# A pitch of 520 columns for buffers of 512: neighbours at different addresses modulo 128 bytes

## The chip, the cores and the metric

The kernel runs on one core of a Trainium2 chip. The metric is the device time of one execution in microseconds. The core has a matrix engine (TensorE: PE in the profile, with its weight loads as PEld), three engines that work on vectors (VectorE: DVE, ScalarE: ACT, GpSimd: POOL) and a queue for transfers (SyncE: SP). They share an on-chip memory of 128 partitions, the SBUF; an address in it is a byte offset within a partition, the same for all 128. TensorE writes to a memory of its own, the PSUM, from which the other engines read.

## The reference

One layer of a hybrid encoder on x of 512 tokens by 2,048 features, all in float32:

```
h = RMSNorm(x);  [q k v u v_sgu gate_a gate_b] = h @ w_in          (2048 x 9216)
branch A: stick-breaking attention, 8 heads of 128, causal, in blocks of 128;  y_a = o @ w_oa
branch B: s = gelu(u) * (W_s LayerNorm(gelu(v_sgu)) + b), in chunks of 128;    y_b = s @ w_ob
x = x + (sigmoid(gate_a) * y_a + sigmoid(gate_b) * y_b) @ w_out
x = x + relu(RMSNorm(x) @ w_ff1)^2 @ w_ff2                          (hidden 8192)
```

## The kernel before

Every large product is made of float32r matmuls in three parts: each operand is split into a rounded part `hi` and a rest `lo`, and `mm3` adds hi x hi, hi x lo and lo x hi (lines 64, 65 and 66). A matmul has a stationary operand of 128 x 128 (loaded by an LDWEIGHTS ahead of it) and a moving operand of 128 partitions by up to 512 columns.

**Buffers.** Two pools of the SBUF hold nearly all that matmuls read:
- 81 *slots* of 512 float32 columns (2,048 bytes), handed out by `slot`. Whatever has 128 x 512 elements is in a slot: the normalised and split activations (`hT_hi`, `hT_lo`, `mT`, `h2T`, `ys` and the like), gates, `relu`, the residual `x2T`, scratch.
- 6 *pieces* of 1,024 columns (4,096 bytes), under the tag `w_piece`: the split weights `w_hi` and `w_lo`, and in `strassen` the sums `w_sum` and the split weights `w_both` (hi in one half, lo in the other).

The raw weights land by DMA in 3 buffers `w_raw` of 1,024 columns. Before the slots and pieces lie small constants, among them the 128 x 128 identity. In the built program the pieces start at byte 34,400 and the slots at byte 60,256, both 96 more than a multiple of 128.

**Work.** `weight` loads a piece of 256 x 512 (for `w_ff1` 512 x 256) weights, copies it to `w_hi` on ScalarE (line 86) and takes `w_lo` as the difference on VectorE (line 88). `by_token` uses slots as the stationary operand and pieces as the moving one; `by_column` the other way about. Both issue 24 matmuls of 512 columns per piece: they make the input projection (q, k, v, ga, vg, u, gb in the profile), `w_oa` (ya), `w_ob` (yb), `w_out` (xo) and `w_ff1` (f). The second product of the MLP is made in 64 blocks by `strassen`: 1,024 x 256 weights in quarters, so seven products of quarters instead of eight, with sums of weights made on GpSimd (line 156, `w_sum`), splits on ScalarE and VectorE (`split_to`, lines 99 and 100, `w_both`), 84 matmuls of 256 columns (q<-ys,w_both), and eight additions of the results to `x2T` on VectorE (line 624). The MLP goes in 8 chunks of 1,024 hidden columns: four pieces of `w_ff1` work (`hidden`), `factors` (sums of activations on GpSimd, split into `ys`) and 8 blocks of `strassen` each; they make up the second half of the time. Small pieces of work between the matmuls (attention, gating, transposes) come from the queue `behind`, one step per weight piece. A list scheduler sets the order of instructions on each engine.

Of the kernel before, what the change touches and what calls it, by code (L numbers as in the profile page):

```python
# [9 lines left out]
F32 = mybir.dt.float32  # L10
F32R = mybir.dt.float32r
# [4 lines left out]
P = 128  # L16
# [7 lines left out]
GROUPS = 8  # L24
DFF = 4 * D
EPS = 1e-6
CK = 2
W = 512

# [2 lines left out]
def tile_hybrid_layer(ctx: ExitStack, tc: tile.TileContext, x, g_mix, w_in, g_q, g_k, ln_g, ln_b,  # L32
# [7 lines left out]
    wpool = ctx.enter_context(tc.tile_pool(name="wpool", bufs=3))  # L40
    small = ctx.enter_context(tc.tile_pool(name="small", bufs=8))
    slots = ctx.enter_context(tc.tile_pool(name="slots", bufs=81))
# [1 line left out]
    ps_aux = ctx.enter_context(tc.tile_pool(name="ps_aux", bufs=3, space=bass.MemoryType.PSUM))  # L44

    def slot(name, dt=F32):
        return slots.tile([P, 512], dt, name=name, tag="slot")

    def acc(name):
        return ps_acc.tile([P, 512], F32, name=name, tag="acc")  # L50

    def aux(name):
        return ps_aux.tile([P, 512], F32, name=name, tag="aux")

    def tiny(n, name):
        return small.tile([P, n], F32, name=name, tag=f"tiny{n}")

    def f32(ap):
        return ap.bitcast(F32)


    def mm3(o, lh, rh, start, stop, **kw):

        nc.tensor.matmul(o, lhsT=lh[0], rhs=rh[0], start=start, stop=False, **kw)  # L64
        nc.tensor.matmul(o, lhsT=lh[0], rhs=rh[1], start=False, stop=False, **kw)  # L65
        nc.tensor.matmul(o, lhsT=lh[1], rhs=rh[0], start=False, stop=stop, **kw)  # L66
# [4 lines left out]
    def step():  # L71
        if behind:
            behind.popleft()()

    def flush():
        while behind:
            step()

    def weight(wap, kt, c0, w=W):

        ck = CK * W // w
        raw = wpool.tile([P, ck, w], F32, name="w_raw", tag="w_raw", bufs=3)
        state["load"] = nc.sync.dma_start(
            out=raw, in_=wap[kt * P:(kt + ck) * P, c0:c0 + w].rearrange("(k p) c -> p k c", p=P))
        hi = wpool.tile([P, ck, w], F32R, name="w_hi", tag="w_piece", bufs=6)
        nc.scalar.copy(out=hi, in_=raw)  # L86
        lo = wpool.tile([P, ck, w], F32R, name="w_lo", tag="w_piece", bufs=6)
        nc.vector.tensor_tensor(out=lo, in0=raw, in1=f32(hi), op=ALU.subtract)  # L88
        return hi, lo

    def split(src, name, scale=None):

        hi, lo = slot(name + "_hi", F32R), slot(name + "_lo", F32R)
        split_to(hi, lo, src, scale)
        return hi, lo

    def split_to(hi, lo, src, scale=None):
        if scale is None:
            nc.scalar.copy(out=hi, in_=src)  # L99
            nc.vector.tensor_tensor(out=lo, in0=src, in1=f32(hi), op=ALU.subtract)  # L100
        else:
            nc.scalar.activation(out=hi, in_=src, func=AF.Copy, scale=scale)
            nc.vector.scalar_tensor_tensor(out=lo, in0=src, scalar=scale, in1=f32(hi),
                                           op0=ALU.mult, op1=ALU.subtract)
# [3 lines left out]
    def by_token(wap, c0, lhs, nk, evac, name):  # L108

        o = [acc(name) for _ in range(NTB)]  # L110
        for kt in range(0, nk, CK):
            hi, lo = early.pop() if early else weight(wap, kt, c0)
            for tb in range(NTB):
                for k in range(CK):
                    a = [part[:, tb * P:(tb + 1) * P] for part in lhs(kt + k)]
                    mm3(o[tb], a, (hi[:, k, :], lo[:, k, :]), kt + k == 0, kt + k == nk - 1)
            step()
        for tb in range(NTB):
            evac(tb, o[tb])

    def by_column(wap, c0, rhs, nk, evac, name, w=W):

        o = [acc(name) for _ in range(w // P)]
        ck = CK * W // w
        for kt in range(0, nk, ck):
            hi, lo = weight(wap, kt, c0, w)
            for c in range(w // P):
                for k in range(ck):
                    a = [part[:, k, c * P:(c + 1) * P] for part in (hi, lo)]
                    mm3(o[c], a, rhs(kt + k), kt + k == 0, kt + k == nk - 1)  # L130
            for _ in range(ck // CK):
                step()
        for c in range(w // P):
            evac(c, o[c])

    def strassen(wap, r0, c0, rhs, evac):

        KH = 4
        half = []
        for h in range(2):
            raw = wpool.tile([P, KH, 2, P], F32, name="w_raw", tag="w_raw", bufs=3)
            state["load"] = nc.sync.dma_start(
                out=raw.rearrange("p k h c -> p k (h c)"),
                in_=wap[r0:r0 + 2 * KH * P, c0:c0 + 2 * P].rearrange("(k h p) c -> h p k c", p=P, h=2)[h])
            half.append(raw)  # L150
        w11, w21 = half[0][:, :, 0, :], half[0][:, :, 1, :]
        w12, w22 = half[1][:, :, 0, :], half[1][:, :, 1, :]
        sums = [wpool.tile([P, 2, KH, P], F32, name="w_sum", tag="w_piece", bufs=6) for _ in range(2)]
        sa, sc, sd, sb = sums[0][:, 0], sums[0][:, 1], sums[1][:, 0], sums[1][:, 1]
        for o, a, b in ((sa, w11, w21), (sc, sa, w22), (sd, sc, w12), (sb, w21, w22)):
            nc.gpsimd.tensor_tensor(out=o, in0=a, in1=b, op=ALU.add)  # L156
        banks = [acc("q") for _ in range(4)]
        for w, name, b, first, last in ((w11, "y11", 0, True, False), (w12, "y21", 1, True, True),
                                        (sa, "m7", 2, True, False), (sc, "m6", 0, False, False),
                                        (sd, "y22", 3, True, True), (w22, "m4", 2, False, True),  # L160
                                        (sb, "m5", 0, False, True)):
            both = wpool.tile([P, 2, KH, P], F32R, name="w_both", tag="w_piece", bufs=6)
            split_to(both[:, 0], both[:, 1], w)
            o = banks[b][:, :2 * P]
            for k in range(KH):
                mm3(o, (both[:, 0, k, :], both[:, 1, k, :]), rhs(k, name), first and k == 0, k == KH - 1,
                    skip_group_check=True)
            evac(name, o)
# [21 lines left out]
    def rsqrt(ms, n, name):  # L190

        r = tiny(n, name)
        nc.gpsimd.tensor_tensor(out=r, in0=ms, in1=mhalf[:, :n], op=ALU.pow)
        return r
# [25 lines left out]
    def load_xk(kt):  # L220

        t = slot("xk")
        nc.sync.dma_start(out=t.rearrange("p (b c) -> p b c", b=NTB),
                          in_=x[:, kt * P:(kt + 1) * P].rearrange("(b p) c -> p b c", p=P))
        for tb in range(NTB):
            xq[tb, kt] = t[:, tb * P:(tb + 1) * P]
        xq[kt] = t

    def load_x(q):

        for tb in range(NTB):
            t = slot("xq")
            nc.sync.dma_start(out=t, in_=x[tb * P:(tb + 1) * P, q * 512:(q + 1) * 512])
            for c in range(4):
                xq[tb, 4 * q + c] = t[:, c * P:(c + 1) * P]
            xq["r", tb, q] = t
# [23 lines left out]
    def scale_of_x():  # L260
        ms = tiny(4, "ms")
        nc.vector.tensor_reduce(out=ms, in_=ss, axis=AX.X, op=ALU.add)
        nc.vector.tensor_scalar(out=ms, in0=ms, scalar1=1.0 / D, scalar2=EPS, op0=ALU.mult, op1=ALU.add)
        nc.gpsimd.tensor_tensor(out=rstd, in0=ms, in1=mhalf, op=ALU.pow)
# [12 lines left out]
    turn_gains(gm, gT)  # L277
    load_xk(1)
    early.append(weight(w_in[0], 0, 0))
    load_xk(2)  # L280
    load_xk(3)
# [12 lines left out]
    def heads_of(c0, g0, half, name):  # L294
# [3 lines left out]
        def evac(tb, o):  # L298
# [6 lines left out]
                                    op=ALU.add)  # L305
            nc.vector.tensor_scalar(out=m, in0=m, scalar1=1.0 / P, scalar2=EPS, op0=ALU.mult,
                                    op1=ALU.add)
# [119 lines left out]
    with tc.issue_after(ref.ins):  # L427
        for half in range(2):
            for src, dst, nm in ((ln_g, lng, "lng"), (ln_b, lnb, "lnb")):
                t = slot(nm)  # L430
# [4 lines left out]
    def normed(tb):  # L435
# [5 lines left out]
        ve = tiny(1, "ve")  # L441
        nc.vector.tensor_scalar(out=ve, in0=mv[:, 1:2], scalar1=EPS, scalar2=None, op0=ALU.add)
        r = rsqrt(ve, 1, "r")
# [23 lines left out]
    with tc.issue_after(ref.ins):  # L467
        ws, bs = [], []
        for half in range(2):
            t = slot("ws")  # L470
# [3 lines left out]
            t = slot("bs")  # L474
# [65 lines left out]
    for j in range(D // W):  # L540
# [7 lines left out]
        with tc.issue_after(ref.ins):  # L548
            for tb in range(NTB):
                t = slot("x2")  # L550
# [17 lines left out]
    nc.vector.tensor_reduce(out=ms2, in_=ss2, axis=AX.X, op=ALU.add)  # L568
    nc.vector.tensor_scalar(out=ms2, in0=ms2, scalar1=1.0 / D, scalar2=EPS, op0=ALU.mult, op1=ALU.add)
    rstd2 = rsqrt(ms2, 4, "rstd2")  # L570
# [38 lines left out]
    for f in range(chunks):  # L609
# [5 lines left out]
        for j in range(D // (2 * P)):  # L615
# [11 lines left out]
            if f == chunks - 1:  # L627
                for pb in range(2):
                    t = aux("xo")
# [36 lines left out]
```

## Time and profile before

| | us |
|---|---|
| median of three timed runs | 2593.71 (2592.04 to 2594.72) |
| the profiled execution's own time | 2592.95 |
| its span, first to last instruction | 2591.2 |
| TensorE busy with matmuls | 2572.0 |
| VectorE / ScalarE / GpSimd busy | 1399.7 / 906.7 / 606.6 |

The lines of the profile are quoted where they are used. A group's row reads: line, engine, operation, written tile <- read tiles, shapes, count | busy time in us, mean ns of one | idle time of the engine just before them, and what ended it. A row of the waits reads: who waited for whom, us in total, times, longest. A row of the windows gives, for a stretch of the span in us, its length, the busy time and count of instructions of the engines shown, the granted TensorE clock, the share of time in which the DMA engines moved data, and GB/s. A row of the timeline gives start and length in us, and in square brackets how long the engine had been idle. Matmul durations include what it takes to get through the array, so they overlap; the spacing of starts is their pace.

### The profile page before, as it was taken

Reading aid. Unit: us, or ns where it says so; the run is one execution under the profiler, and the core shown is the slowest. Engines: PE = TensorE matmul, PEld = TensorE weight load, DVE = VectorE, ACT = ScalarE, POOL = GpSimd, SP = SyncE. Lnnn points to the kernel's source line nnn. Section 1 sums busy time; section 2 is a strip of 40 time slices with the busy share of each in tenths; the row PEclk is TensorE's granted clock in tenths of the full one; section 3 lists DMA queues with packets and bytes.
Section 4 is the critical chain, followed back from the end, with each engine's and each line's share of the span. In section 5 each row is a group of like instructions: output and inputs, shape, how many; then the busy total and the mean of one; then the engine's idle time right before and its main releaser. Section 6 shows DMA issues by size and latency. Waiting matters only on the chain.

```text
span 2591.2 us, 34954 instructions
## 1 busy us (share of the span) xinstructions
PE 2572.0 (99%) x14058; PEld 2235.7 (86%) x14058; DVE 1399.7 (54%) x2030; ACT 906.7 (35%) x1428; POOL 606.6 (23%) x507
## 2 busy tenths in 40 slices
PE   8999999999999999999999999999999999999999
PEld 7888888888888888888899898898998988989989
DVE  4555563333335333333567486584774856847666
ACT  5333342222223222233333343343333433433334
POOL 0211110000201100000143252351522624415233
PEclk9999999999999999999999999999999999999999
DMA  5332322333332333433333333233232332333333
GB/s 171 90 90 74 90 72 91 97 98 98 114 112 84 98 98 98 129 107 107 97 86 115 93 90 114 84 104 110 87 114 90 99 113 83 115 98 90 112 90 117
DMA packets 204419, 260.24 MB, mean 100 GB/s; under 512 B 8368, under 2 KB 146656, under 8 KB 204256
## 3 DMA queue, kind: packets, MB, share of 16 engines
q1 hardware_dynamic: 204256, 258.01, 33.3%
q8 instruction: 110, 1.80, 0.3%
q14 instruction: 53, 0.43, 0.1%
HBM read 253.78 MB, written 4.19 MB: 100 GB/s over the span
## 4 chain that ended last, share of the span: by engine, by line
PE 97%; DVE 2%; issue 0%; DMA 0%; ACT 0%; SPq 0%; POOL 0%; DVEq 0%; ACTq 0%; POOLq 0%
PE q L64 9%; PE q L66 9%; PE q L65 9%; PE f L65 9%; PE f L66 9%; PE f L64 9%; PE xo L66 2%; PE xo L64 2%; PE xo L65 2%; PE gb L64 2%; PE gb L65 2%; PE gb L66 2%; PE ga L64 2%; PE ga L66 2%; PE ga L65 2%; PE v L66 1%
## 5 line engine op out<-in xcount | busy, mean ns | idle before, releaser
L88 DVE TENSOR_TENSOR w_lo<-w_raw,w_hi 128x1024 fp32r<-128x1024 f32 x336 | 415.4, 1236 | 826.5 <-ACT w_hi L86 813.1
L86 ACT CAST w_hi<-w_raw 128x1024 fp32r<-128x1024 f32 x336 | 353.6, 1052 | 951.5 <-PE f L65 248.4
L64 PE MATMUL q<-ys,w_both 128*128 128x256 f32 x1792 | 505.4, 285 | 3.0 <-DVE x2T L624 0.6
L65 PE MATMUL q<-ys,w_both 128*128 128x256 f32 x1792 | 501.8, 283 | 0.1
L66 PE MATMUL q<-ys,w_both 128*128 128x256 f32 x1792 | 491.1, 284 | 3.5 <-DVE w_both L100 3.5
L64 PE MATMUL f<-h2T_hi,w_hi 128*128 128x512 f32 x1024 | 398.7, 389 | 0.0
L65 PE MATMUL f<-h2T_lo,w_hi 128*128 128x512 f32 x1024 | 398.4, 389 | 0.0
L66 PE MATMUL f<-h2T_hi,w_lo 128*128 128x512 f32 x1024 | 397.4, 389 | 0.0
L64 PEld LDWEIGHTS q<-ys,w_both 128*128 128x128 f32 x1792 | 342.9, 191 | 10.4 <-issue 8.9
L65 PEld LDWEIGHTS q<-ys,w_both 128*128 128x128 f32 x1792 | 343.3, 192 | 0.8 <-DVE ys L100 0.3
L66 PEld LDWEIGHTS q<-ys,w_both 128*128 128x128 f32 x1792 | 335.4, 192 | 6.8 <-DVE w_both L100 6.8
L156 POOL TENSOR_TENSOR w_sum<-w_raw 128x512 f32<-128x512 f32 x128 | 185.0, 1452 | 261.3 <-PE q L66 169.1
L624 DVE TENSOR_TENSOR x2T<-x2T,q 128x256 f32<-128x256 f32 x512 | 198.6, 410 | 78.5 <-PE q L66 77.4
L100 DVE TENSOR_TENSOR w_both<-w_raw,w_both 128x512 fp32r<-128x512 f32 x192 | 193.3, 1030 | 67.5 <-ACT w_both L99 67.5
L65 PEld LDWEIGHTS f<-h2T_lo,w_hi 128*128 128x128 f32 x1024 | 192.2, 188 | 39.7
L66 PEld LDWEIGHTS f<-h2T_hi,w_lo 128*128 128x128 f32 x1024 | 192.2, 188 | 39.6
L64 PEld LDWEIGHTS f<-h2T_hi,w_hi 128*128 128x128 f32 x1024 | 192.3, 188 | 39.4
L100 DVE TENSOR_TENSOR w_both<-w_sum,w_both 128x512 fp32r<-128x512 f32 x256 | 217.5, 869 | 1.3 <-ACT w_both L99 1.2
L99 ACT CAST w_both<-w_sum 128x512 fp32r<-128x512 f32 x256 | 157.8, 619 | 171.5 <-PE q L66 133.5
L99 ACT CAST w_both<-w_raw 128x512 fp32r<-128x512 f32 x192 | 118.1, 621 | 227.4 <-PE q L66 113.4
L156 POOL TENSOR_TENSOR w_sum<-w_sum,w_raw 128x512 f32<-128x512 f32 x128 | 183.1, 1431 | 5.0
L596 POOL TENSOR_TENSOR m<-relu 128x256 f32<-128x256 f32 x32 | 37.0, 1158 | 596.7 <-ACT relu L585 596.7
(202 smaller groups left out, 4088.3 us busy)
## 6 DMA issues: line engine op xcount, KB each, us to landing
w_raw<-in_w_ff_dram SPq DMA_DIRECT2D x256, 512.0 KB, 4.0
w_raw<-in_w_in_dram SPq DMA_DIRECT2D x144, 512.0 KB, 3.8
w_raw<-in_w_out_dram SPq DMA_DIRECT2D x32, 512.0 KB, 3.8
w_raw<-in_w_oa_dram SPq DMA_DIRECT2D x16, 512.0 KB, 3.8
w_raw<-in_w_ob_dram SPq DMA_DIRECT2D x16, 512.0 KB, 3.7
x<-in_x_dram SPq DMA_DIRECT2D x16, 256.0 KB, 5.0
out_dram<-out SPq DMA_DIRECT2D x16, 256.0 KB, 4.5
xq<-in_x_dram SPq DMA_DIRECT2D x12, 256.0 KB, 5.5
```

Source lines behind the costliest of these rows:

```text
L64: nc.tensor.matmul(o, lhsT=lh[0], rhs=rh[0], start=start, stop=False, **kw)
L65: nc.tensor.matmul(o, lhsT=lh[0], rhs=rh[1], start=False, stop=False, **kw)
L66: nc.tensor.matmul(o, lhsT=lh[1], rhs=rh[0], start=False, stop=stop, **kw)
L86: nc.scalar.copy(out=hi, in_=raw)
L88: nc.vector.tensor_tensor(out=lo, in0=raw, in1=f32(hi), op=ALU.subtract)
L99: nc.scalar.copy(out=hi, in_=src)
L100: nc.vector.tensor_tensor(out=lo, in0=src, in1=f32(hi), op=ALU.subtract)
L156: nc.gpsimd.tensor_tensor(out=o, in0=a, in1=b, op=ALU.add)
L596: nc.gpsimd.tensor_tensor(out=m7, in0=y12, in1=y22, op=ALU.subtract)
L624: nc.vector.tensor_tensor(out=a, in0=a, in1=o, op=op)
```

## The change

A slot takes room for 520 columns (2,080 bytes) and a piece for 1,040 (4,160 bytes); of each, the first 512 or 1,024 columns are used, as before. 2,080 is 16 x 128 + 32 and 4,160 is 32 x 128 + 64: slot after slot starts 32 bytes further modulo 128, and pieces alternate between two places 64 bytes apart. In the built program pieces start at byte 34,400 and slots at 60,640 (again 96 more than a multiple of 128), so slots stand at 96, 0, 32 and 64 in turn and pieces at 96 and 32. `w_raw` and the constants stay where they were. All of it still fits: the last slot ends at byte 229,120 instead of 226,144. `piece` gives the four kinds of weight pieces the shapes that they had.

On all five engines the instructions stand in the same order, with the same waits and on the same buffers by number; line numbers after the new lines move on by one to five.

```
+PITCH = 520
...
     def slot(name, dt=F32):
-        return slots.tile([P, 512], dt, name=name, tag="slot")
+        return slots.tile([P, PITCH], dt, name=name, tag="slot")[:, :512]
...
+    def piece(name, shape, dt=F32R, **dims):
+        t = wpool.tile([P, 2 * PITCH], dt, name=name, tag="w_piece", bufs=6)
+        return t[:, :2 * W].rearrange(shape, **dims)
...
-        hi = wpool.tile([P, ck, w], F32R, name="w_hi", tag="w_piece", bufs=6)
+        hi = piece("w_hi", "p (k c) -> p k c", k=ck)
...
-        lo = wpool.tile([P, ck, w], F32R, name="w_lo", tag="w_piece", bufs=6)
+        lo = piece("w_lo", "p (k c) -> p k c", k=ck)
...
-        sums = [wpool.tile([P, 2, KH, P], F32, name="w_sum", tag="w_piece", bufs=6) for _ in range(2)]
+        sums = [piece("w_sum", "p (h k c) -> p h k c", F32, h=2, k=KH) for _ in range(2)]
...
-            both = wpool.tile([P, 2, KH, P], F32R, name="w_both", tag="w_piece", bufs=6)
+            both = piece("w_both", "p (h k c) -> p h k c", h=2, k=KH)
```

## The prediction

> **What bounds the kernel now.** I read the page's head first, then who TensorE waits for, then TensorE's pace in stretches of pure work, then the groups of the other engines. Forecast: no measurable change, about 2593.7 us.
>
> The head of the page: span, busy time by engine, granted clock in 40 slices, and the chain that ended last.
>
> ```profile
> span 2591.2 us, 34954 instructions
> PE 2572.0 (99%) x14058; PEld 2235.7 (86%) x14058; DVE 1399.7 (54%) x2030; ACT 906.7 (35%) x1428; POOL 606.6 (23%) x507
> PEclk9999999999999999999999999999999999999999
> PE 97%; DVE 2%; issue 0%; DMA 0%; ACT 0%; SPq 0%; POOL 0%; DVEq 0%; ACTq 0%; POOLq 0%
> ```
>
> TensorE is busy for 2572.0 of 2591.2 us, the last chain is 97% its own matmuls, and the clock is full in every slice. It has one LDWEIGHTS (PEld) for each of its 14,058 MATMULs. The profiled execution took 2592.95 us, 1.75 us more than its span; the median of the three timed runs, 2593.71 us, is 0.8 us above that, so I count from the median.
>
> What TensorE's matmuls wait for (total us, times, longest):
>
> ```profile
> PE xT L256 <- DMA xk<-in_x_dram: 4.7, 2, 3.4
> PE q L66 <- DVE w_both L100: 3.5, 9, 2.0
> PE gp L206 <- DMA gm<-in_g_mix_dram: 2.7, 1, 2.7
> PE q L64 <- DVE x2T L624: 0.6, 2, 0.3
> ```
>
> All of it is 12 us, most of it the loads that the start needs (xk, gm). So the time is the number of matmuls times their pace. The pace from windows (a window's count takes in a matmul that began before it, so I add one duration to the window and divide by the count), first 512-column matmuls alone, then 256-column ones (q, inside one block of `strassen` each):
>
> ```profile
> 860.00:1000.00 140.00, 140.00 (x619) 1.00 0.32 97
> 1546.00:1555.00 9.00, 9.00 (x78) 1.00 0.28 90
> 1566.60:1576.00 9.40, 9.40 (x80) 1.00 0.35 109
> L64 PE MATMUL f<-h2T_hi,w_hi 128*128 128x512 f32 x1024 | 398.7, 389 | 0.0
> L64 PE MATMUL q<-ys,w_both 128*128 128x256 f32 x1792 | 505.4, 285 | 3.0 <-DVE x2T L624 0.6
> L86 ACT CAST w_hi<-w_raw 128x1024 fp32r<-128x1024 f32 x336 | 353.6, 1052 | 951.5 <-PE f L65 248.4
> ```
>
> (140.00 + 0.389) / 619 = 226.8 ns for 512 columns, and (9.00 + 9.40 + 2 x 0.285) / 158 = 120.1 ns for 256. The difference is 0.417 ns per column; 512 columns at that rate are 213.4 ns, so 13.4 ns of every matmul is not columns. There are 336 weight pieces of 24 matmuls in `by_token` and `by_column` (the casts of L86), 8,064 in all, and 3 x 1792 = 5,376 in `strassen`: 13,440 matmuls. 8,064 x 226.8 + 5,376 x 120.1 ns = 1828.9 + 645.7 = 2474.6 us, 95% of the span.
>
> **The change, part by part.** Instructions: none added, none removed, none in another order, no other waits. What changes is where buffers start. Before, slots follow each other at 2,048 bytes and pieces at 4,096, and both pools start 96 bytes past a multiple of 128, so every slot and piece, and every slice that a matmul reads, starts at 96 modulo 128. After, slots step through 96, 0, 32, 64 and pieces alternate between 96 and 32; `w_raw` stays at 96. Both operands of a main matmul come from these two pools (in `strassen`, ys from a slot and w_both from a piece), so about 1 pair in 4 still has equal remainders and 3 in 4, some 10,080 matmuls, do not.
>
> *TensorE's reads.* The question is whether any of the 13.4 ns comes from the two reads (weights and moving columns) starting at the same remainder. The row that is nearest is the attention's three 128-column matmuls, of which the second has its weights loaded while the first streams:
>
> ```profile
> 161.19 0.22 PE L64 MATMUL z<-kT_hi,qT_hi 128*128 128x128 f32 x1
> 161.19 0.19 PEld L65 LDWEIGHTS z<-kT_lo,qT_hi 128*128 128x128 f32 x1
> 161.25 0.28 PE L65 MATMUL z<-kT_lo,qT_hi 128*128 128x128 f32 x1
> 161.30 0.19 PEld L66 LDWEIGHTS z<-kT_hi,qT_lo 128*128 128x128 f32 x1
> ```
>
> The first stream and the next weight load start together at 161.19, both at remainder 96, and the next matmul starts at 161.25. Its 128 columns need 128 x 0.417 = 53.4 ns. To the rounding of these rows that leaves 6.6 ns (0.06 us less 53.4 ns) for everything that a full weight load beside a stream can cost, not 13.4. So the best case is 10,080 x 6.6 ns = 67 us saved, if all of that is the collision. The worst case, if another remainder made reads take turns that don't now: one weight load is at most those 0.06 us long, and with one of the four relative positions bad, 3,360 x 53.4 ns = 179 us lost. I take 0: the 13.4 ns is the same over hundreds of matmuls with the weights on either side (slots as weights in `by_token`, pieces as weights in `by_column` and `strassen`), and in the one place where the two reads start together and nothing else limits, most of it is missing.
>
> By the Trainium skill, "TensorE: Matmul & The Clock Gate", section "Back-to-back issue gap", an isolated 512-column matmul is followed after 518 cycles, 215.7 ns measured; the windows above show 226.8. That page would leave 11 ns per matmul to be explained by something in this kernel; it says itself that pairs with LDWEIGHTS are set by both, and no run here shows a stream without them.
>
> *The vector engines.* Their rows, mean ns of one:
>
> ```profile
> L88 DVE TENSOR_TENSOR w_lo<-w_raw,w_hi 128x1024 fp32r<-128x1024 f32 x336 | 415.4, 1236 | 826.5 <-ACT w_hi L86 813.1
> L624 DVE TENSOR_TENSOR x2T<-x2T,q 128x256 f32<-128x256 f32 x512 | 198.6, 410 | 78.5 <-PE q L66 77.4
> L99 ACT CAST w_both<-w_sum 128x512 fp32r<-128x512 f32 x256 | 157.8, 619 | 171.5 <-PE q L66 133.5
> L450 POOL TENSOR_TENSOR y<-y,lnb 128x512 f32<-128x512 f32 x8 | 10.3, 1290 | 0.5
> L302 POOL TENSOR_TENSOR sq<-k_raw 128x512 f32<-128x512 f32 x8 | 8.4, 1060 | 70.8 <-ACT k_raw L300 70.8
> 1510.00:2430.00 920.00, 917.13 (x5854) 834.57 (x5853) 626.40 (x968) 353.73 (x592) 344.39 (x264) 1.00 0.34 100
> ```
>
> VectorE takes (1236 - 410) / 768 = 1.08 ns per column and ScalarE (1052 - 619) / 512 = 0.85 ns, with both inputs and the output at remainder 96, whether one input comes from SBUF (L624) or two (L88): no sign of a price for equal remainders. GpSimd has one: two different tiles take 1290 ns, the same tile twice 1060. Either way these engines are covered: the last row (busy us of PE, PEld, DVE, ACT, POOL in 920 us of the MLP) has VectorE at 626.40 of 920, ScalarE at 353.73, GpSimd at 344.39, and TensorE at 917.13. What they gain or lose reaches the end at one place only, the start of a block of `strassen`:
>
> ```profile
> 1543.29 1.77 DVE L100 TENSOR_TENSOR w_both<-w_sum,w_both 128x512 fp32r<-128x512 f32 x1
> 1544.98 1.07 DVE L624 TENSOR_TENSOR x2T<-x2T,q 128x256 f32<-128x256 f32 x3
> 1545.51 0.19 PEld L64 LDWEIGHTS q<-ys,w_both 128*128 128x128 f32 x1 [0.24 <-issue]
> L64 PEld LDWEIGHTS q<-ys,w_both 128*128 128x128 f32 x1792 | 342.9, 191 | 10.4 <-issue 8.9
> ```
>
> The split at L100 takes 1.77 us, because GpSimd's w_sum (L156) runs beside it; the first of three x2T additions then ends about 1545.39, and the load of the block's first weights follows at 1545.51 after 0.24 us of idleness. All such idleness is 10.4 us. So a gain on VectorE or GpSimd is worth 10.4 us at most, and a loss costs up to its length times 64 blocks. Value taken: 0, since w_sum's inputs there both lie in w_raw, which isn't moved.
>
> *DMAs.* Weights land in w_raw as before. Only the loads of x and of small tables, and the 16 stores, touch slots:
>
> ```profile
> x<-in_x_dram SPq DMA_DIRECT2D x16, 256.0 KB, 5.0
> xq<-in_x_dram SPq DMA_DIRECT2D x12, 256.0 KB, 5.5
> out_dram<-out SPq DMA_DIRECT2D x16, 256.0 KB, 4.5
> ```
>
> Loads of equal size differ by 0.5 us. TensorE waits twice on xk at the start, and the last store is open at the end: between -1 and +1.5 us (three such half microseconds), taken as 0. The other loads are hidden by TensorE's own queue of work, which never waits for them. Sum: 0 + 0 + 0 on 2593.7 us.
>
> **The rivals.**
> - *Faster, the reads collide now.* For it: 13.4 ns per matmul without a named cause, and equal remainders everywhere. Against: the 128-column pair above, which leaves 6.6 ns at most. Up to 67 us: 2527; half of it, 2560, if the rest is issue; with one column's time (0.417 ns) saved per changed pair only 4.2 us, which doesn't count as faster. Chance 0.10, with 2570 as its middle; the whole 13.4 ns on 10,080 matmuls, 135 us and so 2459, gets 0.02 of it. By the Trainium skill's page named above, the 11 ns that it leaves open would be 10,080 x 11.1 ns = 112 us, an estimate from its figure.
> - *Faster, GpSimd.* If its two-tile price falls towards the same-tile price, 0.23 us off L156 takes the block's idleness with it: at most 10.4 us, 2583. For it: the rows 1290 and 1060. Against: the w_sum that matters has both inputs in w_raw. Chance 0.05.
> - *Slower, one relative position is bad for TensorE.* Weight load and stream run in step now, starting at the same time and the same remainder; they may be clear of each other because of that, and of the three new positions one may not be. It would cost 3,360 matmuls d each, and decides from d = 1.6 ns (5.2 us); with d = 13.4 ns it is 45 us, 2639, and with 4 ns 2607. For it: the pace is even to the nanosecond, so nothing disturbs it now. Against: it needs memory that takes two reads in step but not out of step, and z shows nothing of that kind. Chance 0.11, middle 2605.
> - *It doesn't act at all*: the forecast itself; `w_raw` and PSUM, which most of VectorE's and ScalarE's work reads, aren't moved anyway.
>
> **How the numbers follow.** A change under 0.2% (5.2 us) can't be told from none here: the three runs spread by 2.7 us. No change measurable has 0.73 (0.01 beside it, on the slower side, is for the start's loads); its own range is 2588.5 to 2598.9. Faster 0.15 (0.10 + 0.05), slower 0.12. The predicted time is the likeliest case's, 2593.7 us. The range reaches down to 2575, which takes in the GpSimd case and the upper third of the first rival, and up to 2606, which takes in the lower half of the third: outside lie about 0.07 and 0.06.
>
> **What would show it.** Right: f stays at 389 ns and the window 860 to 1000 at 618 to 620 matmuls; q's pace stays at 120 ns; L86, L88, L99 within 1%; the idleness before q's first LDWEIGHTS near 10 us. The first rival would show as more than 625 matmuls in that window, the third as fewer than 615 or as an uneven pace: slow and fast stretches, by which slot holds the operand. The GpSimd rival shows as a mean of L156 `w_sum<-w_sum,w_raw` clearly under that of `w_sum<-w_raw`, since only the former gets inputs of unequal remainders. I am wrong if the spacing of the 512-column matmuls moves by a single nanosecond: 8,064 of them make that 8 us.

## The result, and the profile after

The changed kernel takes 2629.19 us (median of four runs, 2628.87 to 2630.48) against 2594.22 us: 1.0137 times as long, 95% interval 1.012 to 1.0155. That is 35 us slower, outside the range of 2575 to 2606; the forecast of no change was wrong.

The head of the page of the kernel after: span, busy time, granted clock and chain.

```profile
span 2627.5 us, 34954 instructions
PE 2604.1 (99%) x14058; PEld 2228.7 (85%) x14058; DVE 1400.4 (53%) x2030; ACT 904.6 (34%) x1428; POOL 589.9 (22%) x507
PEclk9999999999999999999999999999999999999999
PE 86%; DVE 12%; issue 2%; DMA 0%; ACT 0%; SPq 0%; POOL 0%; DVEq 0%; ACTq 0%; POOLq 0%
```

TensorE is busy 32.1 us longer with the same 14,058 matmuls under the same clock; VectorE, ScalarE and GpSimd are not. So it is the pace of the matmuls themselves that changed. The windows of the kernel after, first 512-column matmuls, then twice 256-column ones (each stretch free of waits):

```profile
860.00:1000.00 140.00, 140.00 (x606) 1.00 0.30 91
1543.00:1551.50 8.50, 8.50 (x74) 1.00 0.23 68
1563.00:1572.00 9.00, 9.00 (x79) 1.00 0.38 113
```

Counted as in the prediction, 512 columns take (140.00 + 0.394) / 606 = 231.7 ns instead of 226.8, and 256 columns (17.50 + 2 x 0.284) / 153 = 118.1 instead of 120.1. The groups of the kernel after say the same, and name what else moved (lines are five further on):

```profile
L65 PE MATMUL f<-h2T_hi,w_hi 128*128 128x512 f32 x1024 | 403.3, 394 | 0.0
L65 PE MATMUL q<-ys,w_both 128*128 128x256 f32 x1792 | 502.8, 284 | 6.3 <-DVE x2T L629 6.0
L65 PEld LDWEIGHTS q<-ys,w_both 128*128 128x128 f32 x1792 | 337.9, 189 | 14.1 <-issue 12.6
L91 ACT CAST w_hi<-w_raw 128x1024 fp32r<-128x1024 f32 x336 | 352.0, 1048 | 983.3 <-PE f L66 257.0
L93 DVE TENSOR_TENSOR w_lo<-w_raw,w_hi 128x1024 fp32r<-128x1024 f32 x336 | 415.1, 1235 | 853.7 <-ACT w_hi L91 840.6
L455 POOL TENSOR_TENSOR y<-y,lnb 128x512 f32<-128x512 f32 x8 | 10.3, 1293 | 0.5
```

f's matmuls last 394 ns instead of 389. The cast, the difference and GpSimd's sum of two tiles are within 0.5% of before. q's matmuls wait 6.0 us for x2T instead of 0.6, and the idleness ahead of their first weight loads is 14.1 us instead of 10.4. The sum: 8,064 x 4.9 ns = +39.5 us, 5,376 x -2.0 ns = -10.8 us; the other +6.3 us of the measured 35.0 are waits in `strassen` (x2T alone +5.4) and small things.

GpSimd is busy 16.7 us less, nearly all of it in one row, the sums `w_sum<-w_raw`, whose inputs did not move. Its sums in the kernel before (L156) and after (L161):

```profile
L156 POOL TENSOR_TENSOR w_sum<-w_raw 128x512 f32<-128x512 f32 x128 | 185.0, 1452 | 261.3 <-PE q L66 169.1 <-PE f L65 42.7 <-POOL w_sum L156 26.8
L156 POOL TENSOR_TENSOR w_sum<-w_sum,w_raw 128x512 f32<-128x512 f32 x128 | 183.1, 1431 | 5.0
L161 POOL TENSOR_TENSOR w_sum<-w_sum,w_raw 128x512 f32<-128x512 f32 x128 | 182.5, 1426 | 5.0
L161 POOL TENSOR_TENSOR w_sum<-w_raw 128x512 f32<-128x512 f32 x128 | 168.5, 1323 | 278.6 <-PE q L67 161.5 <-issue 45.8 <-PE f L66 44.6
```

### The profile page after: what moved, and what is told of

Read it like the earlier page. It is cut to its first block, busy times and chain, and to the rows that moved or that the text cites. A ratio compares the mean times of both kernels' runs of the same rounds, so it can differ in the third digit from the quotient of the medians.

```text
span 2627.5 us, 34954 instructions
## 1 busy us (share of the span) xinstructions
PE 2604.1 (99%) x14058; PEld 2228.7 (85%) x14058; DVE 1400.4 (53%) x2030; ACT 904.6 (34%) x1428; POOL 589.9 (22%) x507
## 4 chain that ended last, share of the span: by engine, by line
PE 86%; DVE 12%; issue 2%; DMA 0%; ACT 0%; SPq 0%; POOL 0%; DVEq 0%; ACTq 0%; POOLq 0%
PE f L67 9%; PE f L66 9%; PE f L65 9%; DVE w_both L105 9%; PE q L65 6%; PE q L67 5%; PE q L66 5%; DVE x2T L629 2%; PE xo L66 2%; PE xo L65 2%; PE xo L67 2%; PE gb L65 2%; PE gb L67 2%; PE ga L65 2%; PE gb L66 2%; PE ga L67 2%
## 5 line engine op out<-in xcount | busy, mean ns | idle before, releaser
L65 PEld LDWEIGHTS q<-ys,w_both 128*128 128x128 f32 x1792 | 337.9, 189 | 14.1 <-issue 12.6
L66 PEld LDWEIGHTS q<-ys,w_both 128*128 128x128 f32 x1792 | 338.2, 189 | 0.7 <-DVE ys L105 0.3
L67 PEld LDWEIGHTS q<-ys,w_both 128*128 128x128 f32 x1792 | 330.5, 189 | 8.2 <-DVE w_both L105 8.0
L105 DVE TENSOR_TENSOR w_both<-w_raw,w_both 128x512 fp32r<-128x512 f32 x192 | 227.6, 1208 | 70.3 <-ACT w_both L104 70.3
L161 POOL TENSOR_TENSOR w_sum<-w_raw 128x512 f32<-128x512 f32 x128 | 168.5, 1323 | 278.6 <-PE q L67 161.5
L104 ACT CAST w_both<-w_raw 128x512 fp32r<-128x512 f32 x192 | 117.7, 620 | 226.8 <-PE q L67 89.8
L105 DVE TENSOR_TENSOR w_both<-w_sum,w_both 128x512 fp32r<-128x512 f32 x256 | 183.7, 737 | 1.4 <-ACT w_both L104 1.2
L161 POOL TENSOR_TENSOR w_sum<-w_sum,w_raw 128x512 f32<-128x512 f32 x128 | 182.5, 1426 | 5.0
```

## The experiments

There are two theories of the paces: *change of place* (a matmul is slow where its operands start elsewhere than the ones before) and *equal remainders* (it is slow where its two operands, or rather the stream and the weight load beside it, start at unequal remainders). Later there is the question whether the modulus is 128 at all.

**One part alone: slots.** The pieces keep their 1,024 columns.

```
 def piece(...):
-    t = wpool.tile([P, 2 * PITCH], ...)
+    t = wpool.tile([P, 2 * W], ...)
```

> Slots at a pitch of 520 columns, pieces at 1,024 as before. Theory 'change of place': TensorE slows where successive operands start at changing remainders; slots change at every k, so 512-column matmuls are paced at 230 to 232 ns and the time is 2615 to 2630 us. Theory 'equal remainders': a matmul is slow whenever its two operands have unequal remainders; 3 in 4 pairs still do, so the time is that of the full change, 2629 us.

2627.47 us, ratio 1.013 (1.0115 to 1.0146): the cost of the full change within 2 us. Both theories allowed it.

**The other part alone: pieces.** The slots keep their 512 columns.

```
 def slot(...):
-    return slots.tile([P, PITCH], ...)[:, :512]
+    return slots.tile([P, 512], ...)
```

> Pieces at a pitch of 1,040 columns, slots at 512 as before. 'Change of place': pieces change between hi and lo, at every one or two matmuls, so some slowing remains: 2605 to 2625 us. 'Equal remainders': half of the pairs are unequal, two thirds of the full change's cost of 35 us: 2617 us.

2621.97 us, 1.0108 (1.0093 to 1.0123): within the range of *change of place*, and 5 us over the 2617 of *equal remainders*. Each part alone costs most of what both cost, which speaks for a relation between the two pools rather than for how often one pool's starts change, but doesn't settle it. In the windows of the two kernels (slots alone, then pieces alone) the 512-column matmuls have the same pace as in the full change, 606 in 140 us:

```profile
870.00:1010.00 140.00, 140.00 (x606) 1.00 0.32 96
```

```profile
870.00:1010.00 140.00, 140.00 (x606) 1.00 0.32 94
```

**Unequal, and never changing.** The kernel before, with 32 bytes of padding ahead of the slots.

```
+    pad = small.tile([P, 8], F32, name="pad", tag="pad", bufs=1)
+    nc.gpsimd.memset(pad, 0.0)
     def slot(name, dt=F32):
```

> Pitches as before (512 and 1,024 columns), but 32 bytes of padding ahead of the slots, so that every slot starts at 0 and every piece at 96 modulo 128: always unequal, never changing. 'Change of place': 2594 us, within 3. 'Equal remainders': every pair unequal, 35 us times 4/3: 2641 us.

2634.28 us, 1.0157 (1.014 to 1.0174). *Change of place* falls: no remainder changes from matmul to matmul here, and this is the slowest kernel of all (7 us under what *equal remainders* gave). The padding has nothing to do but move the slots. Its window has the fewest matmuls, (140.00 + 0.395) / 602 = 233.2 ns each:

```profile
870.00:1010.00 140.00, 140.00 (x602) 1.00 0.30 92
```

**TensorE alone.** The matmuls without the layer, no other engine at work:

```
 for n in (512, 256):
     for j in range(16):
         stretch(..., n, [(0, 8 * j + P * (i % 3)) for i in range(3)])      # moving at 0, weights 32 j bytes on
```

> The layer is left out (the output is x and other data): 32 stretches of 96 matmuls, float32r, nothing beside them. In 16 stretches of 512 and 16 of 256 columns the moving operand stands still and the weights step by 512 bytes, 32 bytes further in each stretch (wideA to wideP, halfA to halfP); then 5 stretches each in which the weights' start moves by 32, 64, 96, 160 or 256 bytes from matmul to matmul (vwideA to E, vhalfA to E). 'Change of place': wideA to P all at 226 to 228 ns, halfA to P all at 120, vwide at 230 to 234, vhalf at about 118. 'Equal remainders': wideA, E, I, M (equal modulo 128) at 227, the others at 232 or more.

The kernel was run once. The tiles of the two operands, 8,192 bytes each, follow one another, so their starts are taken as equal modulo 256. The groups have 96 matmuls each; the busy time less one duration, over 95, is the pace. The first ten matmuls of wideA start over 400 ns apart, with a granted clock of 1.00 in that window; why is not shown, and wideI, 256 bytes on, stands for it:

```profile
L54 PE MATMUL wideB<-mov,wt 128*128 128x512 f32 x96 | 22.6, 395 | 0.0
L54 PE MATMUL wideE<-mov,wt 128*128 128x512 f32 x96 | 22.5, 394 | 0.0
L54 PE MATMUL wideG<-mov,wt 128*128 128x512 f32 x96 | 22.1, 391 | 0.0
L54 PE MATMUL wideI<-mov,wt 128*128 128x512 f32 x96 | 21.9, 389 | 0.0
L54 PE MATMUL vwideE<-mov,wt 128*128 128x512 f32 x96 | 21.9, 389 | 0.0
L54 PE MATMUL halfA<-mov,wt 128*128 128x256 f32 x96 | 11.7, 283 | 0.0
L54 PE MATMUL halfD<-mov,wt 128*128 128x256 f32 x96 | 11.4, 280 | 0.0
```

wideI is at (21.9 - 0.389) / 95 = 226 ns, wideB (32 bytes off) at 234, and wideE, 128 bytes off and so equal modulo 128, at 233. More exactly, by the spacing of the starts over the last 83 of each stretch, in ns:

| weights less moving, bytes | 0 | 32 | 64 | 96 | 128 | 160 | 192 | 224 |
|---|---|---|---|---|---|---|---|---|
| 512 columns | 226.7 | 233.4 | 233.4 | 234.2 | 232.4 | 233.4 | 228.9 | 233.3 |
| 256 columns | 120.0 | 118.3 | 117.8 | 117.3 | 120.0 | 119.9 | 117.8 | 117.8 |

From 256 bytes on the rows repeat. The theory of equal remainders holds, with two corrections: the modulus is 256, not 128, and for 256 columns equal is not the best. Where the weights' start moves by 256 bytes from matmul to matmul (vwideE) the pace stays at 226.7 ns: a change of place alone costs nothing. The mean over the eight, 232.0 ns and 118.6, lies near the pace of the changed kernel (231.7 and 118.1). It can't be more than near, since the order counts too: stretches that go through all eight differences in turn have 234.1 ns in steps of 32 bytes, 230.8 in steps of 96 and 233.3 in steps of 160. The table also gives the padded kernel, whose differences are 32 or 224 bytes throughout (the slots moved by 32 modulo 256): 8,064 x 6.6 - 5,376 x 2.2 ns = +41 us; measured +40.9. Only the weights' start was swept here, but in the padded kernel only the slots moved, and its matmuls start 233.2 to 233.3 ns apart in k, v, vg and xo, where the slot holds the weights, and 233.3 in u, yb and f, where it holds the stream: what counts is the difference of the two starts.

**Equal modulo 128, not modulo 256.** Slots as before, pieces at 1,056 columns (33 x 128 bytes):

```
-PITCH = 520
+PITCH = 528
 def slot(...):
-    return slots.tile([P, PITCH], ...)[:, :512]
+    return slots.tile([P, 512], ...)
```

> Slots at a pitch of 512 columns, pieces at 1,056 (4,224 bytes, 33 x 128): all starts equal modulo 128, but w_hi and w_lo 128 apart modulo 256. 'Equal modulo 128 is enough': 2594 us. 'Modulo 256': 1 or 2 in 3 of the 512-column matmuls at about 232 ns instead of 226.7, q unchanged at 120: 2609 to 2625 us.

2628.81 us, 1.0134 (1.0118 to 1.0149): equal modulo 128 is not enough. It is slower than the 2609 to 2625 us that I gave the theory modulo 256, and its window has 603:

```profile
870.00:1010.00 140.00, 140.00 (x603) 1.00 0.30 94
```

**The patterns, and steps of 4 bytes.** Do pairs with equal remainders stay fast where others stand between them? And is there a better place than 0? Two kernels of matmuls alone:

```
 for j in range(64):                                      # first kernel: 4-byte steps
     stretch(..., n, [(0, j + P * (i % 3)) for i in range(3)], 48)

 for a, every in {"A": 2, "B": 3, "C": 6, "D": 12, "E": 24, "F": 48}.items():     # second kernel
     stretch("odd" + a, 512, [(0, P * (i % 3) + (32 if i % every == every - 1 else 0)) for i in range(96)])
 ...                                                      # and strassen's order of 12, 4-byte steps
```

> The layer is left out (the output is x and other data): 64 stretches of 48 matmuls of 512 columns and 64 of 256, the weights' start 4 bytes further in each (wideAA, wideAB ... widePP would be 4 bytes a step; the first letter counts 64 bytes). 'Remainders modulo 256': wideAA at 226.7 ns, wideAI, wideBA, wideBI and so on as in the steps of 32 bytes (233, 233, 234, 232, 233, 229, 233), those between near their neighbours; halfAA 120 and 117 to 120 elsewhere. If the collision were of 16-byte lines, four steps in a row would be alike; a remainder with a pace under 226 ns is not expected but would be worth a kernel.

> The layer is left out (the output is x and other data). Six stretches of 96 matmuls of 512 columns with equal remainders, except that every 2nd, 3rd, 6th, 12th, 24th or 48th weight load starts 32 bytes off (oddA to oddF). 'Price by pair': 226.7 ns plus 6.7 ns times the odd share: 230, 229, 228, 227.2, 227 and 226.8. 'Lost step': the equal ones after an odd one run slow too, for some 10 to 15 matmuls, as after the transposes in the kernel before: oddA to oddD at 231 to 233, oddE at 229 to 230, oddF 228 to 229. Then 64 stretches in the order of strassen's 12 matmuls (weights hi, hi, lo; moving halves of four slots) with the weights 0, 4, 8 ... 252 bytes further on (halfAA to halfDP): halfAA at 120, most others at 117 to 120; some settle at 113.3, and the shift whose pace is lowest over 84 matmuls is the one to build into the layer.

In the second, the groups with one weight load in 3, in 6, in 12 and in 48 off by 32 bytes:

```profile
L54 PE MATMUL oddB<-mov,wt 128*128 128x512 f32 x96 | 22.4, 394 | 0.0
L54 PE MATMUL oddC<-mov,wt 128*128 128x512 f32 x96 | 22.1, 392 | 0.0
L54 PE MATMUL oddD<-mov,wt 128*128 128x512 f32 x96 | 22.0, 390 | 0.0
L54 PE MATMUL oddF<-mov,wt 128*128 128x512 f32 x96 | 21.9, 389 | 0.0
```

(22.4 - 0.394) / 95 = 231.6 ns for B, 228.5 for C, 227.5 for D, 226.4 for F. An odd load slows two matmuls: in C to F the starts around it are 232 to 233 and 234 to 235 ns apart, then 227 again. That gives about 226.7 + 2 x 6.7 / 3 = 231.2 in B and 228.9 in C. So neither "price by pair" (229 and 228) nor the "lost step" of 10 to 15 matmuls, which would have left D at 231, is right: the price is per pair, but paid twice. So a third of odd loads costs two thirds of what all of them cost. In the kernel with pieces at 1,056 columns two in three at 232.4 would be 230.5 ns. Its starts are 230.5 to 230.9 ns apart where the pieces are the stream (the projections q, k, v and vg, and xo), but 231.2 to 233.4 where they are the weights (ga, ya, u, gb, yb, f; the window with 232.8 lies there). That part of its cost stays open.

In steps of 4 bytes no stretch of 512 columns was under 226.7 ns, though seven of the 64 starts had it, 0 among them. I had expected the starts between to be near their neighbours; they are not: 132 bytes has 226.7 ns beside 233.5 at 128. Of the eight starts in the table seven come back within 0.2 ns for 512 columns (128 bytes does not), but only three (0, 160 and 192) for 256. Of 256 columns, four starts settled at 113.3 ns (52, 64, 76 and 88 bytes) in the first kernel and five in the second (these and 192). 64 and 192 bytes had been at 117.8 in the steps of 32: some starts have more than one pace. What decides between them is not shown. Three tiles of the second kernel, 0, 76 and 192 bytes off, in strassen's order (shortest/median/longest ns, first to last start in us):

```profile
L54 PE MATMUL halfAA<-mov,wt x84: 277/283/283, 142.0 to 152.0; 128*128 128x256 f32 x84
L54 PE MATMUL halfBD<-mov,wt x84: 276/276/280, 329.8 to 339.2; 128*128 128x256 f32 x84
L54 PE MATMUL halfDA<-mov,wt x84: 276/276/278, 618.3 to 627.7; 128*128 128x256 f32 x84
```

9.4 us for 83 spacings are 113 ns, 10.0 us are 120.

**Into the layer.** The 512-column matmuls want equal remainders, `strassen` does not. Pieces of 1,088 columns (17 x 256 bytes) keep all starts equal modulo 256, and `w_both` alone begins some columns into its piece:

```
+def piece(name, shape, dt=F32R, at=0, **dims):
+    t = wpool.tile([P, 2 * W + 64], dt, name=name, tag="w_piece", bufs=6)
+    return t[:, at:at + 2 * W].rearrange(shape, **dims)
 ...
-            both = wpool.tile([P, 2, KH, P], F32R, name="w_both", ...)
+            both = piece("w_both", "p (h k c) -> p h k c", at=24, h=2, k=KH)       # then 19, then 48
```

> Pieces at a pitch of 1,088 columns (4,352 bytes, 17 x 256), so that all starts stay equal modulo 256, but w_both begins 24 columns (96 bytes) into its piece. 'Modulo 256, and 256 columns the other way about': 512-column matmuls stay at 226.7 ns, q goes from 120.0 to about 117.4: 5,376 x 2.6 = 14 us less, of which the starts of strassen's blocks give some back: 2580 to 2588 us, faster than both. 'Whatever moves a start costs': 2594 us or more.

> As the shift in strassen only, but w_both begins 19 columns (76 bytes) into its piece, where the order of strassen alone settled at 113.3 ns. 'TensorE bounds the blocks': 5,376 x 6.7 ns = 36 us less than before, 2558 us. 'The chain GpSimd, VectorE, TensorE bounds them': q's pace falls to 113 to 115, but the period of a block stays near 10.3 us and the idleness before a block's first weights grows; 2582 to 2591 us.

> The same with 48 columns (192 bytes), which settled at 113.3 ns too, and starts w_both at a multiple of 64 bytes after the other pieces. 'TensorE bounds the blocks': 2558 us. 'The chain bounds them': 2582 to 2591 us, as with 76 bytes within 3 us.

| w_both begins at | us | ratio to before (95%) |
|---|---|---|
| 96 bytes | 2589.81 | 0.9985 (0.9976 to 0.9993) |
| 76 bytes | 2581.03 | 0.9949 (0.9937 to 0.9962) |
| 192 bytes | 2589.03 | 0.9981 (0.9972 to 0.999) |

All three beat the kernel before, if by little (4, 13 and 5 us), and the changed one; with 76 bytes it is the fastest here. The 96 bytes end 2 us over the range of 2580 to 2588 that I gave them. The windows of the kernel with 76 bytes (512 columns; then 256, free of waits) and its groups:

```profile
870.00:1010.00 140.00, 140.00 (x619) 1.00 0.32 98
1523.00:1527.50 4.50, 4.50 (x42) 1.00 0.53 161
1533.00:1537.50 4.50, 4.50 (x42) 1.00 0.52 155
```

```profile
L64 PE MATMUL f<-h2T_hi,w_hi 128*128 128x512 f32 x1024 | 398.7, 389 | 0.0
L64 PE MATMUL q<-ys,w_both 128*128 128x256 f32 x1792 | 495.7, 280 | 12.8 <-DVE x2T L628 12.7
L64 PEld LDWEIGHTS q<-ys,w_both 128*128 128x128 f32 x1792 | 336.4, 188 | 23.1 <-issue 19.5
```

f is where it was. q is paced at (9.00 + 2 x 0.28) / 84 = 113.8 ns, 6.3 ns under before, worth 34 us; 13 arrive. Of the rest, the idleness ahead of q's weight loads has taken 12.7 us (23.1 against 10.4), and the wait for x2T another 12.1 (12.7 against 0.6; the two overlap in part). From the timeline of this kernel:

```profile
1520.89 0.68 DVE L104 TENSOR_TENSOR w_both<-w_sum,w_both 128x512 fp32r<-128x512 f32 x1
1521.48 0.28 PE L66 MATMUL q<-ys,w_both 128*128 128x256 f32 x1
1521.50 1.07 DVE L628 TENSOR_TENSOR x2T<-x2T,q 128x256 f32<-128x256 f32 x3
1522.02 0.19 PEld L64 LDWEIGHTS q<-ys,w_both 128*128 128x128 f32 x1 [0.46 <-issue]
1522.05 0.36 PE L64 MATMUL q<-ys,w_both 128*128 128x256 f32 x1 [0.29 <-DVE x2T L628]
```

The load waits for the first of three additions on VectorE, 0.46 us where it was 0.24. It is not at the start of a block, as the prediction has it: counted from the block's first, it is the 61st of 84 matmuls, the first of the product m4, which adds to the bank of m7 once VectorE has read m7 from it; that reading is the first of the three additions, held up behind VectorE's splits. So the second of the two theories holds for the most part: the chain through VectorE takes back over half of the gain, and the time ends 1 us under the range given for it. The 192 bytes, which I expected within 3 us of the 76, are 8 us slower: they stayed near 118 ns in the layer (median spacing of q's starts; 113 with 76 bytes), another case of two paces for one start.

## Why the prediction was wrong

- **What bounds the kernel: right.** TensorE's pace times the number of matmuls; its last paragraph even has the scale, "a single nanosecond ... 8 us". It moved by 4.9.
- **TensorE's reads, "I take 0": the step that failed.** The pairs lost the equal remainders that gave the 512-column matmuls their best pace. I read the evenness of the pace ("the weights on either side", the same 13.4 ns) as a sign that places don't matter; but every row of the kernel before had the same place, so evenness could show nothing of the kind. The z row has the same flaw: it too is a pair at equal remainders, of 128 columns, and bounds what such a pair can gain. It says nothing of unequal ones, and nothing of longer streams: in the kernel after, the eight pairs of this kind start 57 to 60 ns apart, as before. Its bounds of -67 and +179 us were honest; taking 0 between them, and 0.73 for it, was not supported by any row. The runs show +39.5 us for the 512-column matmuls in its place.
- **The third rival was the mechanism, mis-sized.** "One relative position is bad" for 3,360 matmuls: the alone-kernel shows 7 of 8 positions bad, by 2.2 to 7.5 ns, so all 8,064 pay 4.9 on average; and it gave this rival 0.11. That is +39.5 us, inside the rival's +5 to +45, but from more than twice the matmuls at a smaller price than its 13.4 ns.
- **Missed: 256 columns go the other way.** 5,376 x -2.0 ns, -10.8 us, stand in neither part of the sum.
- **"About 1 pair in 4 still has equal remainders": wrong** in the modulus. It is 256, so 1 in 8; and an equal pair behind an unequal one is slow too.
- **The vector engines, 0: right** for the rows that the prediction named, and the GpSimd rival did not act: its sign was `w_sum<-w_sum,w_raw` clearly under `w_sum<-w_raw`, and it is now above. What moved is the row whose inputs stayed in place, from 1452 to 1323 ns; it is also at 1314 in the padded kernel and 1313 with 76 bytes, and why is not shown. The waits in `strassen` grew as TensorE got faster there, which the cover of "626.40 of 920" hid. The idle load that the prediction shows at 1545.51 is not at the start of a block either: it belongs to the 61st of the 84 matmuls, as in the kernel with 76 bytes.
- **DMAs, 0:** nothing of them is among what TensorE waits for beyond the start.

## What to carry to other kernels

Where TensorE is the bound and every matmul loads its weights, the byte addresses of the two operands are a tuning parameter, here worth 1 to 3% of a 512-column matmul in float32r: keep them equal modulo 256 for 512 columns, and measure a few shifts for shorter streams, in the order of the real kernel. Padding that is meant to spread buffers should be a multiple of 256 bytes unless it is measured. An even pace in a trace in which a quantity never varies is no evidence on that quantity: a stretch of matmuls alone, with that quantity swept, answers it in one run.

## What the runs showed of the hardware

- With every matmul loading its weights, the pace of TensorE depends on where the weights start relative to the stream, with no other engine at work: 226.7 to 234.2 ns for 512 columns, repeating after 256 bytes in steps of 32 (up to 237.3 in steps of 4).
- For 256 columns most starts have 115.5 to 122.2 ns, equal ones 120.0; a few have 113.3, and 28 to 36 bytes have 133.3 in the steps of 4 bytes alone. The same start can have two paces. Less the columns (256 x 0.417 = 106.7 ns) 113.3, 120.0 and 133.3 leave 6.6, 13 and 27 ns. What in TensorE or the SBUF makes these steps is not settled by these runs.
- Among equal loads, one that is 32 bytes off slows two 512-column matmuls, by 13.4 ns together, and no more.
- The Trainium skill, "TensorE: Matmul & The Clock Gate", section "Step-by-step: what each phase is for", has it that loading the next weights takes no read bandwidth from the running matmul, since the two reads have ports of their own. The stretches alone differ by 3% (226.7 to 234.2 ns) with nothing but the weights' start changed, so here the measurement decides: ports of their own or not, where the next weights start changes the pace of the matmuls. The pace of 215.7 ns on that page was reached by no stretch of 512 columns; all of them load weights for each matmul.
